# A six-layer encoder trunk on one core: a planner of weight work is replaced by one written order of all instructions and written buffer places

## The chip, the cores and the metric

One core of a Trainium2 chip runs the whole program as one launch. The metric is the device time of one execution in microseconds (us). For the kernel before it is the median of three runs, and one further execution was taken with the hardware profiler; its trace is the source of every view shown here.

The engines go by their short names in the profile's rows: PE is TensorE (PEld its weight loads, which overlap its matmuls), DVE is VectorE, ACT is ScalarE, POOL is GpSimd, SP is the engine that only issues transfers. In the trace each engine's instructions start in the order in which the program issued them; between engines there are semaphores. So an instruction that waits holds back all that stand behind it on its engine.

## The reference, cut to what matters

Two layers, 256 tokens of width 1024, all float32. Each layer has three stages, so there are six in all:

```
for l in range(DEPTH):                                        # DEPTH = 2
    x = LN(ALPHA * x + 0.5 * swiglu(x, ffn_w_in[l, 0], ffn_w_out[l, 0]))
    x = LN(ALPHA * x + mixer_l(x))                            # l = 0: mLSTM, l = 1: window attention
    x = LN(ALPHA * x + 0.5 * swiglu(x, ffn_w_in[l, 1], ffn_w_out[l, 1]))

def swiglu(x, w_in, w_out):                                   # w_in 1024 x 5632, w_out 2816 x 1024
    gu = x @ w_in
    g, u = gu[..., :D_FF], gu[..., D_FF:]
    return (jax.nn.silu(g) * u) @ w_out
```

The order of the stages is thus ffn, mLSTM, ffn, ffn, attention, ffn. Nothing of the mathematics changes here.

## The kernel before, in words

**Splitting.** A float32 operand is held as two parts of the faster type fp32r: `hi`, a rounded copy, and `lo`, what is left. A product is three matmuls (`mm3`): hi by hi, hi by lo, lo by hi. For activations, ScalarE makes `hi` and VectorE makes `lo` straight from the PSUM bank (`split_evac`). For weights the same is done with tiles of 128 x 1024: a load brings 512 KB into a raw tile, ScalarE copies it to `w_hi` (line 204, with a scale line 206), VectorE subtracts to get `w_lo` (line 222, with a scale line 224). Ten places each for `w_hi` and `w_lo` (`RING = 10`) hold weights that are ready for PE; a place comes free when PE has used its tile.

**The ffn stage.** The first 512 columns of g and u are plain products. Most other columns go by a scheme of seven products in place of eight (`seven`): it needs sums of weight blocks, which are made in place in the raw tiles, on VectorE (`tensor_add`, line 236) or by an accumulating transfer issued from POOL (line 240), and sums of transposed inputs (the tiles `S1` to `S4`). Between the products stand blocks of the down projection (`down`, tiles `py`), whose input `h` is silu(g)*u (tile `hh` or `u0`, `u1`), transposed on PE and split again. The stage ends with six down blocks and the layer norm (`tail`, `Norm`).

**Three queues beside PE.** PE's matmuls stand in the order in which the Python code calls them. All other work of the weights is placed between them by a planner that runs while the program is built. The class `Counted` counts every instruction that the model's own code issues. After each one `Weights.run` looks at four lists, H (a `w_hi`), L (a `w_lo`), S (a sum on VectorE) and A (an accumulating transfer); the string `ORDER` gives for each of them the count at which it is due:

```
early = self.made < upto or self.half and self.half[0][0] < upto
next_ = [(o[0], what) for what, o in self.order.items()
         if o and (early or o[0][0] <= self.nc.n) and self.ready(what)]
```

Within one list the order is fixed: `w_lo` tiles are made in the order in which PE will use them. The model's own instructions on VectorE, ScalarE and POOL (evacuations, copies, sums of inputs, norms) stand in the order of the code and cannot pass each other; only weight work is set between them.

**Loads.** SP issues a load as soon as a raw place is free (`Weights.load`, called from `low` and `sum`): four places `w_raw` that live through the whole program, and in an ffn stage six places `s_raw` and two `v_raw` out of that stage's pool. `W.open(pool, end)` at the start of an ffn stage gives those eight to the planner, so before that point only the four `w_raw` places take loads of the coming stage. Each stage has its own pool (`tc.tile_pool(name="ffn")` and so on), closed at its end; four PSUM banks carry the tag `pw` and four `py`, each handed out in turn.

**Names.** `load_x` brings the four halves of the input on ScalarE's queue; `to_xT` transposes x into `xT`; `pending` is the transposing of the second token half, which the next stage does after its first matmuls; `proj`, `scores`, `turn`, `values` and `out_proj` are the parts of the attention stage, `mix`, `divide`, `combine` and `settle` those of the mLSTM. Nearly all instructions bear line 94, a helper that issues them, so they are told apart by their tiles.

Of the kernel before, what the change touches and what calls it, by code (L numbers as in the profile page):

```python
# [1 line left out]

# [27 lines left out]
S_RAW = 6  # L30
V_RAW = 2
RING = 10
QC = [5, 16, 22, 27, 32]
# [5 lines left out]

ORDER = (  # L40
    "H19L0H16L0H33L3H2L4H3H7L2H2L1L5H38H9L0L1S6H2L4H2L0S0H3H3H5L3L3H5L1L12S3S0A8A5H8L3A4H2L2A2H0H2L1H2H0H0H0H0L4L12"
    "L4L3L2L7H6H0H7L2H2H2L1H3L0H1L1S0S0L18H0L7A3A0L6L7H3S17L0S17H3H3L1H0H1A3L4A2L3H2H0H0H2L2H1L3L9L4H1L1L2H7H6L5L7H"
    "2L3L8H2H3H1L4L1H9L3H2L5H11L1L1H1H2L0S2H1A23H5L0S2L0L1H1S2L0A1H5S13H0L3A5H7L1A0H0H1L11L3H8H5L1L4L5H5L1H11L2H2L2"
    "H0H4L2H4H10L6S3H11L2L9L0H0H1S2H1L2A1L3A2S13L5H6L1S8H0H2A6H0L9L4H1H5L1H2L2H2L3L6A5L4H0H0H8H4L2L6L1L14H16H0L2L0H"
    "6H0L1H0L8L11H27L3H14L7H6H6H16L4L1L2H4L2H66H13L30L8H12H6L0H6H47L2H1L6H38L1H1H1L16L15L11H12H5H0L6H13L2L10L15L3H8"
    "H7L40L7H55L8H101L53H60L1H2L0H0H31H1L0L1H4L0L0H0H47L11L11H56H0H0L0L10L0H5L0H6H4L22L4H43L10H1H0L5S1H6L10H11H1L2L"
    "4S9A7L0H0S4L7A4H13S1L5A5H2H4L1A0H3L2H2H3L3H1H2H2L8H3L1L4L1L0H3H19L2L3H0L2L0S2S2H1L4H0H2H17H9L1L8A9L1A4S3L1S5H1"
    "2L4H0H0H1A3L4A2L3H2H0H0L4H3L1H0L9H0L4L2L2H14H10L3L10H9H1L1H0H1L1L1L2H5L2H3L5H5H4L4L1S0H1S3H1L0H14H8A1L3L0L1L0S"
    "2A6H1S2L3H9A11L8A0H0H1L12H2L6H2L0H5L5L5H0H3L3H11H0H0L2L4L10H0L4H6L4L9H6H6S1H1L2S0L0H0L2L0A7A5S9H0S1L14H12A5H2H"
    "7L2L1H2L5H0H3L2L5L6H1A4H4H0H0L8H8L4L4L0L12H15L0H1L0H7H0L1H0L14H1L4L12H32L7H11L3H14L4H0L1H5L16H44L22H2H2L3H0L0L"  # L50
    "6H24L7S3H5S2L5S4A10H1L2A2S12H10H1L3A4L4H1A1L3H0H0H5L1L4H1H5L3H1L4L1L2H13H0L8H0H3L2H2L1L2L1S0S0H14L2H1H3H9L10L2"
    "A3A10L5S0S8H16H0H0L1A2H0L4A2L3H2H0H0H0H0L4L4L9L4H2L5L3H7H4L4H0L6H0L2L1L20H1L1H2L2H2H5L5L11H10H3L1H2H6S1H3A5L2S"
    "1L1L0L1H0S1A6L6H8L7A5S3H3L2H0A0H0H1L1L1L0H20H5H3L2L5L6H11H0H0H0L2L4L10H0L5L2H3L4H19H3L5S0H5A2S0L0L1H0S2A2H9L9L"
    "3S0H15H2A3L0L4H5H5L5H0L5L5H5L1A5H4H0H0H11L1H3L6L2L2L6H18H1H0H1L2L0L7H11L8L7H23L13H14H5L10L2H2H4L6L1H31L5H22H38"
    "L2L2H14L8H21L24H35H0H3L6H1L9L2H41L18H7L14L33H36L27H54L9H37L33H19L27H25L27H80L18H24L4H18H2L4L3H4L18H59H5H3L2L1L"
    "0H1L5H9L6S15H3S14H4L0S2A7L4A1S1H21L4H0H4A0L4H1A1L3H2H0H0H0H0L4L4L9L4L1H2L0H14H8L2H1L2L3L0S2H1H1L7L3H4H3L0S1H4L"
    "13L4A4S5A5S0H29H0H0L1A2H0L4A2L3H2H0H1H1H1L1L4H2L7L4L2H15L1L3H2L9L2H2H14L1L0H0L1H0L3H7H5L5H1L4S0L1H1L6H0H4L18H2"
    "A5S5L0L0S1A6H5L0H3L1A17S2H4L2A0H0L1H0H1L0L11H10H5L5H2L3L6H4H7H0L2H3L1L10H0L6L3S0H1H0H15S3L4L9L0A7A5H3L1S2H3H4L"
    "5L15S0H3H5A0L0H9L3H2L5H0H4L1H1L4L6A5H4H0L5H2H9L4L2L10L2H15H2H0L1L8L0"
)  # L60


class Counted:


    def __init__(self, nc):
        self.nc, self.n, self.then = nc, 0, None
        for name in ("tensor", "vector", "scalar", "gpsimd"):
            setattr(self, name, Engine(self, getattr(nc, name)))

    def __getattr__(self, name):
        return getattr(self.nc, name)

    def load(self, ap, source, engine=None):
        if engine is not None:
            engine.dma_start(ap, source)
        elif isinstance(source, list):
            for k, src in enumerate(source):
                self.nc.sync.dma_start(ap[:, k].rearrange("p (m f) -> p m f", m=src.shape[1]), src)
        else:  # L80
            self.nc.sync.dma_start(ap, source)


class Engine:
    def __init__(self, counted, engine):
        self.counted, self.engine = counted, engine

    def __getattr__(self, name):
        f, c = getattr(self.engine, name), self.counted
        if name.startswith("preload") or "dma" in name:  # L90
            return f

        def call(*args, **kw):
            r = f(*args, **kw)  # L94
            c.n += 1
            if c.then is not None:
                c.then()
            return r
        return call


class Weights:

    def __init__(self, nc, pool, words, plan, after):
        self.nc, self.pool, self.words, self.plan, self.after = nc, pool, words, plan, after
        self.raw, self.parts, self.half = {}, {}, []  # L110
        self.sums = {"S": [], "A": []}
        self.made = self.used = self.room = 0
        self.todo = {tag: [i for i, w in enumerate(words) if w["tag"] == tag] for tag in ("w_raw", "s_raw")}
        self.free = {"w_raw": RAW_BUFS, "v_raw": 0, "s_raw": 0}
        self.spool, self.send = None, 0
        self.uses = [0] * len(words)
        self.order, n = {what: [] for what in "HLSA"}, 0
        for i, (what, step) in enumerate(re.findall(r"([HLSA])(\d+)", ORDER)):
            n += int(step)
            self.order[what].append((n, i))  # L120
        for p in plan:
            self.uses[p["word"]] += 1
        for sums in after.values():
            for w, v in sums:
                if isinstance(v, int):
                    self.uses[v] += 1
        self.first = {}
        for i, p in enumerate(plan):
            self.first.setdefault(p["word"], i)
            for _, v in after.get(i, ()):  # L130
                if isinstance(v, int):
                    self.first.setdefault(v, i + 0.5)

    def open(self, pool, end):

        self.spool, self.send = pool, end
        self.free["s_raw"], self.free["v_raw"] = S_RAW, V_RAW
        self.load()

    def load(self, most=None):  # L140

        nc = self.nc
        n = 0
        while most is None or n < most:
            next_ = []
            for tag, todo in self.todo.items():
                local = todo and todo[0] < self.send
                in_ = tag if self.free[tag] else "v_raw"
                if todo and (local or tag == "w_raw") and (in_ == tag or local and tag == "w_raw") and self.free[in_]:
                    next_.append((self.first[todo[0]], tag, in_))  # L150
            if not next_:
                break
            _, tag, in_ = min(next_)
            i = self.todo[tag].pop(0)
            pool, bufs = {"w_raw": (self.pool, RAW_BUFS), "v_raw": (self.spool, V_RAW), "s_raw": (self.spool, S_RAW)}[in_]
            t = pool.tile([128, D], F32, name=tag, tag=in_, bufs=bufs)
            nc.load(t.rearrange("p (k f) -> p k f", k=self.words[i]["k"]), self.words[i]["src"])
            self.raw[i], self.words[i]["in"] = t, in_
            self.free[in_] -= 1
            n += 1  # L160

    def drop(self, w):
        self.uses[w] -= 1
        if not self.uses[w]:
            del self.raw[w]
            self.free[self.words[w]["in"]] += 1

    def ready(self, what):
        if what == "L":
            return bool(self.half)  # L170
        if what in self.sums:
            q = self.sums[what]
            return bool(q) and all(w in self.raw for w in q[0][1:] if isinstance(w, int)) and not any(
                x[0] == q[0][0] for x in (self.sums["S"] if what == "A" else ()))
        p = self.plan[self.made] if self.made < min(self.room, len(self.plan)) else None
        return p is not None and p["word"] in self.raw and not any(
            x[0] == p["needs"] and (len(x) == 2 or x[1] == p["word"])
            for x in self.half + self.sums["S"] + self.sums["A"])

    def run(self, upto=0):  # L180

        while True:
            early = self.made < upto or self.half and self.half[0][0] < upto
            next_ = [(o[0], what) for what, o in self.order.items()
                     if o and (early or o[0][0] <= self.nc.n) and self.ready(what)]
            if not next_:
                assert not early, (self.made, self.used, self.nc.n)
                break
# [4 lines left out]
    def high(self):  # L193
# [14 lines left out]
        self.made += 1  # L208

    def low(self):  # L210

        nc = self.nc.nc
        i, hi = self.half.pop(0)
        p = self.plan[i]
# [1078 lines left out]
```

## Time and profile before

| what | value |
|---|---|
| median of 3 runs | 936.27 us (934.73 to 937.51) |
| the profiled execution, its own time | 935.19 us |
| its span, first to last instruction | 933.4 us |
| busy: PE, PEld, DVE, ACT, POOL | 914.4, 756.3, 812.3, 574.3, 147.0 us |
| instructions on PE, DVE, ACT, POOL | 4368, 955, 813, 202 |
| moved from memory | 206.65 MB, 223 GB/s over the span |

How to read it: the matmuls overlap each other, so that one of 512 columns stays in flight for about 0.39 us while the next starts 0.23 us after it. PE therefore counts as busy through most of its short waits, and its 98% is not a measure of how much it waits. The weight loads (PEld) do not overlap in that way; their waits are the better list of the moments at which PE had nothing to do.

### The profile page before, as it was taken

What the parts mean: (1) busy time and instruction counts of PE and PEld (TensorE: products, weight loads), DVE (VectorE), ACT (ScalarE), POOL (GpSimd) and SP (SyncE); (2) the same over time, 40 slices, a digit from 0 to 9 for tenths busy, and PEclk for the clock granted to TensorE, in tenths of its full rate; (3) what the DMA queues carried; (4) which work ended last, traced back from release to release, by engine and by line L of the source; (5) the groups of instructions that cost most, each with busy time, mean ns of one, the idle gap of its engine ahead of it and who ended that gap; (6) DMA issues with size and microseconds to landing.
All of it is one profiled execution on the core that took longest, in us unless ns stands there. A gap on an engine that the chain in (4) does not pass through costs nothing.

```text
span 933.4 us, 12378 instructions
## 1 busy us (share of the span) xinstructions
PE 914.4 (98%) x4368; PEld 756.3 (81%) x4368; DVE 812.3 (87%) x955; ACT 574.3 (62%) x813; POOL 147.0 (16%) x202
## 2 busy tenths in 40 slices
PE   9999999999999999999999999999999999999996
PEld 7788888789988788888887888887887787888885
DVE  6899988987687999899889999888888889989986
ACT  6576576546664576765645765765578556676670
POOL 0131111010210112012011111020534302102110
PEclk9999999999999999999999999999999999999999
DMA  8999997646624989998767998975652177999941
GB/s 286 322 274 264 305 270 177 202 136 193 215 99 133 340 235 223 345 254 236 209 209 242 289 258 280 303 154 181 204 177 95 56 285 174 296 314 230 311 116 45
DMA packets 100637, 208.50 MB, mean 223 GB/s; under 512 B 6848, under 2 KB 21200, under 8 KB 100576
## 3 DMA queue, kind: packets, MB, share of 16 engines
q1 hardware_dynamic: 82368, 173.04, 52.9%
q0 software_dynamic: 17632, 33.64, 21.6%
q10 hardware_dynamic: 576, 1.05, 0.3%
q8 instruction: 34, 0.56, 0.2%
q14 instruction: 27, 0.22, 0.1%
HBM read 206.65 MB, written 1.05 MB: 223 GB/s over the span
## 4 chain that ended last, share of the span: by engine, by line
PE 75%; DVE 12%; DMA 5%; ACT 4%; issue 2%; POOL 0%; SPq 0%; DVEq 0%; ACTq 0%
PE pw L94 48%; PE py L94 28%; DVE w_lo L222 5%; DMA s_raw<-in_ffn_w_in_dram 2%; ACT w_hi L204 2%; DVE s_raw L236 1%; DMA w_raw<-in_ffn_w_out_dram 1%; DVE e L94 1%; ACT sc L94 1%; DVE S L94 1%; DVE h_lo L94 1%; DVE rm L94 1%; DVE S_lo L94 0%; DVE o L94 0%; DVE h L94 0%
## 5 line engine op out<-in xcount | busy, mean ns | idle before, releaser
L204 ACT CAST w_hi<-s_raw 128x1024 fp32r<-128x1024 f32 x192 | 197.4, 1051 | 112.6 <-DVE s_raw L236 83.9
L222 DVE TENSOR_TENSOR w_lo<-w_raw,w_hi 128x1024 fp32r<-128x1024 f32 x211 | 253.1, 1219 | 11.0 <-ACT w_hi L204 10.3
L222 DVE TENSOR_TENSOR w_lo<-s_raw,w_hi 128x1024 fp32r<-128x1024 f32 x192 | 229.5, 1220 | 24.3 <-ACT w_hi L204 23.7
L204 ACT CAST w_hi<-w_raw 128x1024 fp32r<-128x1024 f32 x211 | 214.3, 1050 | 44.8 <-DMA w_raw<-in_ffn_w_out_dram 9.8
L94 PE MATMUL pw<-w_hi,xT_hi 128*128 128x512 f32 x480 | 191.4, 399 | 0.7 <-ACT w_hi L204 0.7
L94 PE MATMUL pw<-w_hi,xT_lo 128*128 128x512 f32 x480 | 187.6, 391 | 0.0
L94 PE MATMUL pw<-w_lo,xT_hi 128*128 128x512 f32 x480 | 187.2, 390 | 0.1
L240 POOL DMA_DIRECT2D s_raw<-in_ffn_w_in_dram x64 | 77.7, 1227 | 477.8 <-DVE s_raw L236 183.2
L94 PE MATMUL py<-w_hi,h_hi 128*128 128x512 f32 x352 | 138.3, 393 | 0.3 <-ACT h_hi L94 0.3
L94 PE MATMUL py<-w_hi,h_lo 128*128 128x512 f32 x352 | 137.7, 391 | 0.7 <-DVE h_lo L94 0.6
L94 PE MATMUL py<-w_lo,h_hi 128*128 128x512 f32 x352 | 137.6, 391 | 0.1
L94 PEld LDWEIGHTS pw<-w_hi,xT_lo 128*128 128x128 f32 x480 | 90.1, 188 | 19.5
L94 PEld LDWEIGHTS pw<-w_lo,xT_hi 128*128 128x128 f32 x480 | 90.4, 188 | 18.2 <-DVE w_lo L222 0.9
L94 PEld LDWEIGHTS pw<-w_hi,xT_hi 128*128 128x128 f32 x480 | 90.2, 188 | 18.2 <-ACT w_hi L204 1.1
L94 PE MATMUL pw<-w_lo,S_hi 128*128 128x512 f32 x256 | 100.3, 392 | 1.1 <-DVE w_lo L222 1.1
L94 PE MATMUL pw<-w_hi,S_hi 128*128 128x512 f32 x256 | 99.7, 390 | 0.0
L94 PE MATMUL pw<-w_hi,S_lo 128*128 128x512 f32 x256 | 99.7, 389 | 0.0
L94 PEld LDWEIGHTS py<-w_hi,h_lo 128*128 128x128 f32 x352 | 66.1, 188 | 16.1 <-DVE h_lo L94 2.6
L94 PEld LDWEIGHTS py<-w_lo,h_hi 128*128 128x128 f32 x352 | 66.1, 188 | 15.2 <-DVE w_lo L222 1.8
L236 DVE TENSOR_TENSOR s_raw<-s_raw 128x1024 f32<-128x1024 f32 x64 | 77.4, 1219 | 0.4
L94 PEld LDWEIGHTS py<-w_hi,h_hi 128*128 128x128 f32 x352 | 66.1, 188 | 13.9 <-ACT h_hi L94 0.7
L94 PEld LDWEIGHTS pw<-w_lo,S_hi 128*128 128x128 f32 x256 | 48.1, 188 | 12.8 <-DVE w_lo L222 3.0
(218 smaller groups left out, 1142.3 us busy)
## 6 DMA issues: line engine op xcount, KB each, us to landing
s_raw<-in_ffn_w_in_dram SPq DMA_DIRECT2D x96, 512.0 KB, 7.3
w_raw<-in_ffn_w_out_dram SPq DMA_DIRECT2D x88, 512.0 KB, 6.7
w_raw<-in_ffn_w_in_dram SPq DMA_DIRECT2D x64, 512.0 KB, 5.0
s_raw<-in_ffn_w_in_dram POOLq DMA_DIRECT2D x64, 512.0 KB, 7.5
w_raw<-in_ml_w_in_dram SPq DMA_DIRECT2D x24, 512.0 KB, 4.0
w_raw<-in_ffn_w_in_dram SPq DMA_DIRECT2D x32, 256.0 KB, 6.9
w_raw<-in_at_w_in_dram SPq DMA_DIRECT2D x12, 512.0 KB, 4.1
w_raw<-in_ml_w_out_dram SPq DMA_DIRECT2D x8, 512.0 KB, 4.1
```

The costliest lines, as they stand in the source:

```text
L94: r = f(*args, **kw)
L204: nc.scalar.copy(hi, raw)
L222: nc.vector.tensor_sub(lo, raw, hi.bitcast(F32))
L236: nc.vector.tensor_add(t, t, self.raw[v])
L240: nc.gpsimd.dma_start(t.rearrange("p (k f) -> p k f", k=self.words[w]["k"]), v, accum_op=OP.add)
```

## The change

Every engine call of the model code is now only written down (`Program.ops`), and `Program.issue` at the very end issues all of them in the order given by the string `ORDER`, which is now a list of steps through the 6,654 calls. `Weights.split` writes down the `hi` copy, the `lo` subtraction and the sums of a tile at the point of its use; where they land among the other instructions is settled by `ORDER` alone. The planner (`Weights.run`, `ready`, `high`, `low`, `sum`, `done`, `open`) is gone.

Buffers come from `Rooms`: a buffer has a list of places, and the string for its kind in `SLOTS` names the place of each use in turn (without a string, the places are taken round and round). The eight PSUM banks are one kind, `p`. Raw tiles are one kind per stage: the four `w_raw` places, and in ffn stages eight `s_raw` places beside them. `Stage` puts a stage's buffers at fixed addresses in one region that all stages share, without opening or closing a pool; two neighbouring stages of the same kind (the third and the fourth, both ffn) use the very same buffers. An instruction that overwrites an address waits for the last user of that address, whichever stage it belongs to.

Set side by side in program order, the two programs have the same instructions (calls, by the program's own count): 4368 on PE, 955 on VectorE, 785 on ScalarE, 198 on POOL and 348 transfers on SP's queue. All 4368 matmuls and transposes stand in the same order as before. On VectorE 842 instructions stand at another place in the queue, the mean shift being 3.5 places and the largest 47; on ScalarE it is 691, on POOL 98, on SP 296.

```diff
-S_RAW = 6
-V_RAW = 2
+S_RAW = 8
 RING = 10
+PLACES = {"ffn": (("h_hi", 1024, 2, FR), ("h_lo", 1024, 2, FR))}
+WHOLE = 21800
 ORDER = (
-    "H19L0H16L0H33L3H2L4H3H7L2H2L1L5H38H9L0L1S6H2L4H2L0S0H3H3H5L3L3H5L1L12S3S0A8A5H8L3A4H2L2A2H0H2L1H2H0H0H0H0L4L12"
...
+    "0 5 35 -34 63 -65 4 1 75 -74 1 109 -108 1 87 -99 13 1 123 -135 13 1 136 21 -156 1 1 1 3 1 -3 4 1 -25 189 "
...
+SLOTS = {
...
+    "stats": ("010101010101"),
...
+class Program:
     def __init__(self, nc):
-        self.nc, self.n, self.then = nc, 0, None
-        for name in ("tensor", "vector", "scalar", "gpsimd"):
+        self.nc, self.ops = nc, []
+        for name in ("tensor", "vector", "scalar", "gpsimd", "sync"):
             setattr(self, name, Engine(self, getattr(nc, name)))
+    def issue(self):
+        at, order = 0, []
+        for step in ORDER.split():
+            at += int(step)
+            order.append(at)
...
+        for i in order:
+            f, args, kw = self.ops[i]
+            f(*args, **kw)
...
+        f, ops = getattr(self.engine, name), self.program.ops
+        return lambda *args, **kw: ops.append((f, args, kw))
+class Rooms:
...
+    def take(self, name, shape, dt):
+        places, slots, k = kind = self.kinds[name]
+        kind[2] += 1
+        at = places["0123456789abcdefghijkl".index(slots[k])] if slots else places[k % len(places)]
...
+class Stage:
...
+        places = [self.bass.alloc_sbuf_tensor_at(key.replace(".", "_") + f"_{k}", [128, n], dt,
+                                                 offset=self.start + 4 * (at + k * step)).ap() for k in range(bufs)]
...
 class Weights:
-    def run(self, upto=0):
-        while True:
-            early = self.made < upto or self.half and self.half[0][0] < upto
...
+    def split(self, i):
+        nc, p = self.nc, self.plan[i]
+        k, scale, raw = p["k"], p["scale"], self.load(p["word"])
+        hi = self.rooms.take("w_hi", [128, D], FR)
+        lo = self.rooms.take("w_lo", [128, D], FR)
...
+            nc.scalar.copy(hi, raw)
+            nc.vector.tensor_sub(lo, raw, hi.bitcast(F32))
...
     def take(self, n):
-        i = self.used
         self.used += n
-        self.run(self.used)
-        return [self.parts[j] for j in range(i, i + n)]
+        return [self.split(i) for i in range(self.used - n, self.used)]
...
-    wpool = ctx.enter_context(tc.tile_pool(name="weights", bufs=RING))
+    raws = tiles("w_raw", D, F32, RAW_BUFS)
+    rooms.kind("w_hi", tiles("w_hi", D, FR, RING))
+    rooms.kind("w_lo", tiles("w_lo", D, FR, RING))
+    rooms.kind("p", tiles("p", 512, F32, 8, psum))
...
+    for j, (kind, *_) in enumerate(stages):
+        if j and kind == stages[j - 1][0]:
+            keys.append(keys[-1])
+            stage_rooms.append(stage_rooms[-1])
+        else:
+            keys.append(str(j))
+            stage_rooms.append(new_stage(kind, keys[-1]))
...
-        return psum.tile(list(shape), F32, name="pw", tag="pw", bufs=4)
+        return rooms.take("p", list(shape), F32)
...
-            pool = ph.enter_context(tc.tile_pool(name="ffn", bufs=1))
+            pool = stage_rooms[bound[0]]
...
     pending()
+    nc.issue()
```

More of the change, by code (lines that the diff above doesn't have):

```diff
@@ L84 @@
[L84 to L99, printed above, removed]
-class Weights:
[L108 to L178, printed above, removed]
-    def run(self, upto=0):
-        while True:
-            early = self.made < upto or self.half and self.half[0][0] < upto
[L184 to L188, printed above, removed]
-            _, what = min(next_)
-            self.order[what].pop(0)
-            self.high() if what == "H" else self.low() if what == "L" else self.sum(what)
-    def high(self):
-        nc, i = self.nc.nc, self.made
-        p = self.plan[i]
-        scale, raw = p["scale"], self.raw[p["word"]]
-        hi = self.pool.tile([128, D], FR, name="w_hi", tag="w_hi", bufs=RING)
@@ new lines, with __init__, load @@
+class Weights:
+    def __init__(self, nc, rooms, words, plan, after):
+        self.nc, self.rooms, self.words, self.plan, self.after = nc, rooms, words, plan, after
+        self.raw, self.used = {}, 0
+    def load(self, i):
+        if i not in self.raw:
+            w = self.words[i]
+            self.raw[i] = t = self.rooms.take(w["room"], [128, D], F32)
+            t = t.rearrange("p (k f) -> p k f", k=w["k"])
+            if isinstance(w["src"], list):
+                for k, src in enumerate(w["src"]):
+                    self.nc.sync.dma_start(t[:, k].rearrange("p (m f) -> p m f", m=src.shape[1]), src)
+            else:
+                self.nc.sync.dma_start(t, w["src"])
+        return self.raw[i]
+    def split(self, i):
[3 more added lines that the diff above has]
+        lo = self.rooms.take("w_lo", [128, D], FR)
@@ L251, in done @@
-    def done(self, upto=None):
-        upto = self.used if upto is None else upto
-        for j in [j for j in self.parts if j < upto]:
-            del self.parts[j]
-        self.room = max(self.room, upto + RING)
-        self.run()
+        return [self.split(i) for i in range(self.used - n, self.used)]
 @with_exitstack
@@ L333, in seven @@
         downs(3)
-    ends = {}
     for j, (kind, l, i, _) in enumerate(stages):
+        now[0] = j
         if kind == "ffn":
@@ L379, in trunk_kernel @@
                 rows(at_w_out[0], c)
-        ends[j] = len(words)
     xt = [state.tile([128, D], F32, name=f"x{t}", tag=f"x{t}") for t in range(2)]
@@ L621, in ffn @@
                             early[4 * m + a]()
-                        W.done()
                     if m == 0:
-                        W.open(pool, ends[bound[0]])
                         for t in range(2):
@@ L627, in ffn @@
             else:
-                W.open(pool, ends[bound[0]])
                 for t in range(2):
@@ L770, in ffn @@
                     small_loads()
-            gb = load_ln(lambda name: pool.tile([128, D], F32, name=name, tag="s_raw", bufs=S_RAW), l, n)
+            gb = load_ln(lambda name: rooms.take(f"raw.{keys[bound[0]]}", [128, D], F32), l, n)
             norm = [Norm(t, 2 * ALPHA, 4 * LN_EPS, gb, last) for t in range(2)]
-            todo = list(zip(range(2 * UNITS - TAIL, 2 * UNITS), W.take_rows(TAIL)))
+            todo = list(zip(range(2 * UNITS - TAIL, 2 * UNITS), W.take(TAIL)))
             return tail(y, lambda c, t: pair(hT[c], A, tok(t)), (todo, todo), False, norm,
@@ L1238, in attn @@
                     lows.append((d, o))
-                held = [wo[c][0] for c in wo if c not in CT]
-                W.done(min([W.used - (2 if qpart else 0)] + held))
                 if st < 8:
```

217 lines of the change are left out of this document (120 added, 97 removed), and 189 rows, old and new, of the table ORDER.

## The prediction

> **What bounds the kernel now.** I read the page first, then the chain of what ended last, then the waits of PE's weight loads, then the timelines of the places where PE waits.
>
> ```profile
> span 933.4 us, 12378 instructions
> ...
> PE 914.4 (98%) x4368; PEld 756.3 (81%) x4368; DVE 812.3 (87%) x955; ACT 574.3 (62%) x813; POOL 147.0 (16%) x202
> ```
>
> PE is the bound, and VectorE, idle for 121 us of the span, is close behind. The change leaves PE's instructions and their order alone, so the time can only change by PE's waits and by what follows its last matmul. The busy 98% hides the waits. The chain gives the pace of undisturbed matmuls and the end of the program:
>
> ```profile
> 377.03 2.72 PE py L94 x12
> ...
> 916.39 9.56 PE py L94 x42
> ...
> 925.98 0.70 DVE x L94
> ```
>
> Twelve matmuls of 512 columns take 2.72 us, 0.23 us each. The last ones end near 925.96; the 7.4 us from there to the end of the span are the second half of a norm on VectorE and the stores, the same instructions afterwards. Now the waits of PE's weight loads over the whole span (us in total, times, longest):
>
> ```profile
> PEld pw L94 <- DVE w_lo L222: 3.9, 8, 1.1
> PEld pw L94 <- DVE pr_lo L94: 3.2, 8, 0.7
> PEld py L94 <- DVE h_lo L94: 2.6, 5, 1.1
> PEld pw L94 <- issue: 2.5, 5, 1.0
> PEld pw L94 <- ACT w_hi L204: 2.0, 2, 1.1
> PEld py L94 <- DVE w_lo L222: 1.8, 4, 0.6
> PEld pw L94 <- DVE ident L94: 1.4, 1, 1.4
> PEld pw L94 <- ACT e L94: 1.3, 1, 1.3
> PEld py L94 <- ACT q_hi L94: 1.3, 1, 1.3
> PEld pw L94 <- DVE hh L94: 1.2, 1, 1.2
> PEld py L94 <- ACT h L94: 1.1, 1, 1.1
> PEld py L94 <- DMA x<-in_x_dram: 1.0, 1, 1.0
> PEld py L94 <- DVE w_lo L224: 0.9, 1, 0.9
> PEld pw L94 <- POOL sc L94: 0.9, 1, 0.9
> PEld py L94 <- ACT h_hi L94: 0.7, 1, 0.7
> ```
>
> The fifteen rows are 41 waits and 25.8 us. A weight load can begin while the matmul before it still streams, so I count each wait 0.23 us shorter for PE: 25.8 - 41 x 0.23 = 16.4 us lost. Two waits, for `ident` and for the first half of x (1.9 us by the same count), are the start itself. **14.5 us**, 1.6% of the span, is all that a better order of the other queues can win.
>
> **The change part by part.** Instructions and bytes are equal; raw places are 12 in an ffn stage before and after (4 + 6 + 2 against 4 + 8), and the ten places of `w_hi` and `w_lo` and the eight banks stay. What changes is who stands ahead of whom. For each losing place I give its most, by the count above, and what I take of it.
>
> *The first product, 25 to 50 us.* The waits of this window alone, and VectorE's timeline in it:
>
> ```profile
> PEld pw L94 <- DVE w_lo L222: 2.5, 3, 1.1
> ```
> ```profile
> 29.72 1.22 DVE L236 TENSOR_TENSOR s_raw<-s_raw 128x1024 f32<-128x1024 f32 x1
> 30.85 0.68 DVE L94 TENSOR_TENSOR hh<-sg,pw 128x512 f32<-128x512 f32 x1
> 31.45 1.22 DVE L222 TENSOR_TENSOR w_lo<-s_raw,w_hi 128x1024 fp32r<-128x1024 f32 x1
> ```
>
> With the `hh` wait of 1.2 that lies here, 3.7 us in four waits: 2.8 us lost. The `w_lo` begun at 31.45, for which PE waits, has 25 instructions ahead of it on VectorE; in the written order it has 18. Six of the instructions that make S1 to S4 and the first `hh`, at 0.68 us as `hh`, and the sum of 1.22 us go behind it (one short copy comes ahead): 7 x 0.68 + 1.22 = 6.0 us out of its way, against a wait of at most 1.1. The other waits of the window get room in the same manner. I take 2.3 of 2.8, the rest being transfers that run at full load here (below).
>
> *Entry into the ffn stages at 326, 503 and 775 us.* PE waits for the second `hh`. In the list these are `ACT e` 1.3, one `ACT w_hi` and one `issue` of about 1.0 each, and after each a wait of 0.4 under `py`, `w_lo`: 4.5 us in six waits, 3.1 us lost. The timeline of VectorE has the `hh` of the first of them, SP's shows the loads before it, and two windows the load on the transfers (busy us of PE, PEld, DVE, ACT and POOL, then the clock, the transfers' busy share and GB/s):
>
> ```profile
> 325.20 0.68 DVE L94 TENSOR_TENSOR hh<-sg,pw 128x512 f32<-128x512 f32 x1
> ```
> ```profile
> 306.86 1.90 SPq L81 DMA_DIRECT2D s_raw<-in_ffn_w_in_dram  x4
> ```
> ```profile
> 250.00:300.00 50.00, 48.79 (x258) 41.27 (x257) 40.53 (x80) 25.10 (x46) 5.55 (x5) 1.00 0.31 105
> 300.00:325.00 25.00, 25.00 (x117) 20.53 (x115) 22.99 (x28) 14.48 (x19) 2.76 (x2) 1.00 0.95 319
> ```
>
> The stage's `s_raw` places are opened only at 306.86; before that the transfers are busy for 0.31 of the time, after it for 0.95. In the written order the first of these eight places takes a load 11 places earlier in SP's queue, ahead of a load of the mLSTM's output weights, once the mLSTM's last use of that address is over. So VectorE can have weight work in its idle time (9.5 us in 250 to 300, 2.0 us in 300 to 325). It needs that: in the new order `hh` has more work ahead of it than before, by 2.0, 2.7 and 1.4 us at the three places (splits and a sum come forward, S instructions go back). PE gains only if the idle time is filled by more than that. Since the idle time is about five times as much, I take 2.0 of 3.1. If it is not filled, the same figures turn into a loss: see the second rival.
>
> *The ends of the ffn stages* (`h_lo` 2.6, the other `w_hi` 1.1, `h_hi` 0.7, the fourth `py` `w_lo` 0.6: 5.0 us in eight waits, 3.2 lost). Here the result of the last product has to pass through ScalarE, VectorE, PE's transposes and both again; in the chain of the last stage two pieces of it read
>
> ```profile
> 908.87 0.69 DVE e L94
> ...
> 909.57 0.60 DVE h_lo L94
> ```
>
> and no order shortens these; it can only see to it that nothing stands before them. I take 1.0.
>
> *mLSTM* (`h` 1.1, `w_lo` line 224 0.9: 1.5 lost). The `w_lo` in question stands three places earlier in VectorE's queue. I take 0.8.
>
> *Attention* (`pr_lo` 3.2, `q_hi` 1.3, `sc` 0.9, the other `issue` 1.5: 6.9 us in fourteen waits, 3.7 lost).
>
> ```profile
> 700.00:725.00 25.00, 24.93 (x130) 19.86 (x130) 21.80 (x43) 22.61 (x67) 12.68 (x25) 1.00 0.30 93
> ```
>
> ScalarE is busy for 22.6 of 25 us, VectorE for 21.8, and each step needs the one before; the orders of both queues hardly differ here (the second `pr_lo` of the waits near 721 us is VectorE's instruction 744 before and 742 after). I take a quarter, 0.9. The other `pw`, `w_lo` waits (1.4 us in five) are 0.2 us by the count: nothing.
>
> *The start gets something worse.* Four transfers bring x on ScalarE's queue; then ScalarE evacuates the first transposes; PE needs the last two halves at 10.63.
>
> ```profile
> 0.79 2.20 ACTq L76 DMA_DIRECT2D x<-in_x_dram  x4
> ...
> 5.63 0.58 ACT L94 CAST xT_hi<-py 128x512 fp32r<-128x512 f32 x1 [1.32 <-PE py L94]
> ```
> ```profile
> 10.63 1.04 PE L94 MATMUL py<-ident,x 128*128 128x128 f32 x8
> ```
> ```profile
> DMA to landing us min/median/max: 3.6/6.2/7.8
> ```
>
> In the written order the transfer of the second half of the first 128 tokens stands behind that evacuation, so it is issued not before 5.63 + 0.58 = 6.2 us. Behind it in the queue stand the first `hi` copies, which wait for the issue alone. By the landing times of the four it arrives at 9.8, 12.4 or 14.0: PE waits 0, 1.8 or 3.4 us. I take 1.0, between the best and the median, because three of the four have landed by then and less is in flight. The Trainium skill ("DMA: Bandwidth & Descriptors", Queues, rings and completion order) says that each transfer engine takes turns between the rings of the queues that have work, so that a late transfer on ScalarE's ring need not wait behind SP's weight loads; by that rule the term would be 0 and the time 1 us less. The landing times above, with both rings loaded, do not decide it.
>
> *Free of cost:* POOL's order. Its moved memsets and the norm's power step are under 2 us each, and PE never waits for POOL but for `sc`. If that cover were gone, the power step at a stage's end would hold the norm by one memset.
>
> The sum: 2.3 + 2.0 + 1.0 + 0.8 + 0.9 - 1.0 = 6.0 us less in the span, 927.4. The profiled execution took 935.19 us, 1.8 more than its span, and lies 1.1 below the median of 936.27; against the median I forecast 936.27 - 6.0 = **930.3 us**.
>
> **The rivals.** (What a measurement can tell from no change is about 0.3%, 2.8 us.)
>
> 1. *Nothing gained:* waits go round. Freed waits come back on the next late operand, as ScalarE's `hi` copies are what VectorE's `w_lo` wait for, and attention gives nothing. Half of the recoverable terms and the start's full 3.4: 936.27 - 3.5 + 3.4 = 936.2. For it: PE's small waits have seven different releasers in the list. Against: the two largest losing places have one clear cause each. It includes the case that the shared addresses make a stage wait for the last user of the one before, so that the early loads come no earlier. 14%.
>
> 2. *Slower: evacuations stuck behind weight work.* The order now lets a split stand in front of an `hh`, `e` or `h_lo` that PE needs sooner, counting on the load being there. Where a load lands late, PE waits for the split too. At the three entries that is 2.0 + 2.7 + 1.4 = 6.1 us, and in each of the four ffn stages some four evacuations stand behind one more split than before; at 1.22 us each, half of it felt, 4 x 4 x 0.61 = 9.8. With nothing won but the first product and the entries hit: 936.27 - 2.3 + 1.0 + 6.1 = **941.1**; with the 9.8 as well, 951. It decides itself where transfers are busy for 0.95 of the time, as in 300 to 325: if the earlier loads only push others back. Against it: between 250 and 300 there is room for them. 17%.
>
> 3. *The start fails alone:* 3.4 us there, the rest as forecast: 932.7. 7%.
>
> 4. *Nearly all waits go:* 12 of the 14.5 and no loss at the start: 924.3. An order of all four queues leaves room for it; the chains at the stage ends and in attention speak against. 10%.
>
> **How the numbers follow.** The forecast has 52%; it runs from 927 (attention and the stage ends at a half) to 933 (entries and mLSTM nothing). Cases 3 and 4 are faster too. So faster by over 0.3%: 52 + 7 + 10, less a little of the forecast's upper edge, 0.68. Within 0.3%: rival 1 and that edge, 0.15. Slower: 0.17. The range from 922 (all 14.5 won) to 942 takes in rival 2 at its 941.1, and leaves out its worse cases and little else.
>
> **What would show it.** Right: in the list of PE's weight-load waits, `w_lo` falls from 3.9 to near 1.5 and the `hh`, `e` rows vanish; the first `s_raw` load of the third stage goes out before 300 us; transfers in 250 to 300 are busier than 0.31; DVE's busy time stays 812. The x wait grows by at most 2 us. Attention's `pr_lo` row stays near 3. Wrong: if the sum of the list stays above 23 us, or if `hh` waits grow at 326, 503 or 775 (rival 2), or if the program's time moves while the list does not, since then PE's pace of 2.72 us for twelve matmuls changed, for which I see no reason.

## The result: slower by half a per cent, although PE waits less

| | time before | time after | ratio (95% interval) |
|---|---|---|---|
| median of 7 runs each | 937.51 us | 941.66 us | 1.0048 (1.0028 to 1.0067) |
| profiled execution, its span | 933.4 us | 937.9 us | |

The forecast was 930.3 us, faster; the kernel became 4.2 us slower. The page of the kernel after begins:

```profile
span 937.9 us, 12265 instructions
PE 921.9 (98%) x4368; PEld 757.3 (81%) x4368; DVE 814.0 (87%) x955; ACT 578.4 (62%) x813; POOL 142.3 (15%) x202
```

PE is busy for 7.5 us more than before (914.4) with the same 4368 matmuls. The waits of its weight loads (us in total, times, longest) became shorter in sum, as was forecast:

```profile
PEld p L301 <- DVE pr_lor L301: 4.7, 10, 1.6
PEld p L301 <- DMA x<-in_x_dram: 2.8, 2, 1.8
PEld p L301 <- POOL sc L301: 1.8, 3, 1.2
PEld p L301 <- ACT q_hir L301: 1.7, 2, 0.9
PEld p L301 <- DVE ident L301: 1.5, 1, 1.5
PEld p L301 <- DVE w_lo L301: 1.2, 2, 0.7
PEld p L301 <- ACT t L301: 1.1, 2, 0.8
PEld p L301 <- DVE t L301: 0.8, 4, 0.2
```

The whole list, with four rows of under 0.8 us that are left out here, is 17.4 us in 33 waits; the whole list before, the prediction's fifteen rows and two smaller ones, was 26.5 us in 43. The waits for `pr_lo`, x, `sc` and `q_hi` grew. (`hh`, `e` and `sg` are called `t` now, `h_hi` is `h_hir`, both `pw` and `py` are `p`.) So fewer waits and more time: the pace of PE itself has changed. The timeline of PE in the kernel after shows it in four microseconds (start, duration, operation). Of the two operands behind the arrow the second is stationary, a weight load (PEld) has brought it; the first streams through PE, the moving operand. Here the activations are stationary and the model's weights move:

```profile
61.72 0.40 PE L301 MATMUL p<-w_hi,xT_lo 128*128 128x512 f32 x1
61.95 0.39 PE L301 MATMUL p<-w_hi,h_hir 128*128 128x512 f32 x1
62.19 0.40 PE L301 MATMUL p<-w_lo,h_hir 128*128 128x512 f32 x1
...
64.52 0.39 PE L301 MATMUL p<-w_hi,h_lor 128*128 128x512 f32 x1
64.75 0.39 PE L301 MATMUL p<-w_hi,xT_hi 128*128 128x512 f32 x1
...
65.88 0.39 PE L301 MATMUL p<-w_hi,xT_lo 128*128 128x512 f32 x1
```

The twelve matmuls whose stationary operand is `h` take 2.80 us from 61.95 to 64.75, 0.233 us each; the five steps with `xT` behind them take 1.13 us, 0.226 each. The kernel before, at the same place:

```profile
62.72 0.39 PE L94 MATMUL py<-w_hi,h_hi 128*128 128x512 f32 x1
...
65.44 0.39 PE L94 MATMUL pw<-w_hi,xT_hi 128*128 128x512 f32 x1
```

Twelve `h` steps in 2.72 us, 0.227 each. Over the whole trace, taking the distance from one start to the next for all 512-column matmuls and leaving out those of 260 ns and more (a wait), the 1797 steps into a matmul with `h` or `S` as stationary operand average 233.3 ns after and 227.1 before; the 1434 into one with `xT` stay at 227.6 (227.9 before). That is 1797 x 6.2 ns = 11.2 us. From PE's first start to its last the program takes 3.84 us more; so everything else on PE, its waits above all, became 7.3 us shorter. Behind PE's last matmul there are 0.64 us more, from this piece of the chain:

```profile
931.52 0.16 DVE rs L301
...
931.79 0.96 POOLq L1440
...
932.77 1.43 DVE x L301 x2
...
934.22 0.75 DVE x L301
```

and before:

```profile
927.67 0.15 DVE rs L94
...
927.83 0.72 DVE x L94 x2
...
929.07 0.74 DVE x L94
```

In the kernel before both halves of the norm's first step (the x2) run on VectorE while GpSimd takes the power; in the written order one of them stands behind it. 11.2 - 7.3 + 0.64 = 4.5 us, the difference of the spans.

### The profile page after: what moved, and what is told of

Read it like the earlier page. It is cut to its first block, busy times and chain, and to the rows that moved or that the text cites. A ratio compares the mean times of both kernels' runs of the same rounds, so it can differ in the third digit from the quotient of the medians.

```text
span 937.9 us, 12265 instructions
## 1 busy us (share of the span) xinstructions
PE 921.9 (98%) x4368; PEld 757.3 (81%) x4368; DVE 814.0 (87%) x955; ACT 578.4 (62%) x813; POOL 142.3 (15%) x202
## 3 DMA queue, kind: packets, MB, share of 16 engines
q10 hardware_dynamic: 576, 1.05, 0.3%
HBM read 206.65 MB, written 1.05 MB: 221 GB/s over the span
## 4 chain that ended last, share of the span: by engine, by line
PE 93%; DMA 2%; DVE 2%; ACT 2%; POOL 0%; issue 0%; POOLq 0%; ACTq 0%
PE p L301 93%; DMA x<-in_x_dram 1%; DMA s_raw<-in_ffn_w_in_dram 1%; DVE pr_lor L301 0%; ACT w_hi L301 0%; ACT sc L301 0%; DVE rm L301 0%; DVE x L301 0%; DVE o L301 0%; POOL sc L301 0%; DVE nm L301 0%; ACT q_hir L301 0%; ACT o L301 0%; DVE w_lo L301 0%; POOL sm L301 0%
## 5 line engine op out<-in xcount | busy, mean ns | idle before, releaser
L301 ACT CAST w_hi<-w_raw 128x1024 fp32r<-128x1024 f32 (+1 forms) x168 | 174.3, 1046 | 85.2 <-PE p L301 43.3
L301 DVE TENSOR_TENSOR w_lo<-w_raw,w_hi 128x1024 fp32r<-128x1024 f32 (+1 forms) x168 | 202.4, 1218 | 27.6 <-ACT w_hi L301 27.3
L301 PE MATMUL p<-w_hi,xT_hi 128*128 128x512 f32 x512 | 203.7, 398 | 0.0
L301 PE MATMUL p<-w_hi,xT_lo 128*128 128x512 f32 x512 | 200.1, 391 | 0.0
L301 PE MATMUL p<-w_lo,xT_hi 128*128 128x512 f32 x512 | 199.7, 390 | 0.3 <-DVE w_lo L301 0.3
L301 PE MATMUL p<-w_hi,h_hir 128*128 128x512 f32 x320 | 127.3, 398 | 0.0
L301 PE MATMUL p<-w_lo,h_hir 128*128 128x512 f32 x320 | 126.4, 395 | 0.0
L301 PE MATMUL p<-w_hi,h_lor 128*128 128x512 f32 x320 | 126.2, 395 | 0.0
L301 PE MATMUL p<-w_hi,S_hir 128*128 128x512 f32 x256 | 101.3, 396 | 0.4 <-ACT t L301 0.4
L301 PE MATMUL p<-w_lo,S_hir 128*128 128x512 f32 x256 | 101.2, 395 | 0.0
```

## The experiments

**Is it the place of the tiles?** What distinguishes `h` and `S` from `xT` after the change is where they begin. In the built programs the weights, PE's moving operand, begin at a remainder of 96 bytes modulo 256 in both kernels, and so does `xT`. `h` and `S` begin at remainder 96 in the kernel before and at 64 after it, because the region that all stages share begins there. Three kernels move nothing but places (the second also issues one small memset on GpSimd).

```diff
-WHOLE = 21800
+WHOLE = 21856          # changed kernel: the region starts 224 bytes lower
```

> The changed kernel with its shared stage region begun 224 bytes lower, so that the stage buffers stand at the address remainder (96 of 256 bytes) that they had in the kernel before; the order of issue and the waits in the program are untouched. In the traces, 1823 matmuls whose stationary operand is h or S start 233.3 ns apart after the change against 227 ns before, and those with xT stay at 227. Theory P (place: the pace of a matmul follows from where its stationary tile begins): the h and S matmuls return to 227 ns, 1823 x 6.4 ns = 11.6 us come back, 941.7 - 11.6 = 930 us, while PE's waits stay as in the changed kernel. Theory O (order: the slower pace comes from what the other engines now do beside PE): the pace stays near 233 ns and the time near 941 us.

```diff
           state.tile([128, 8, S], FR, name="xT_lo", tag="xT_lo"))
+    pad = state.tile([128, 56], F32, name="pad", tag="pad")      # kernel before: 224 bytes
+    tc.nc.gpsimd.memset(pad[:, 0:1], 0.0)
```

> The kernel before with one unused 224-byte buffer ahead of its stage pools, so that h and S begin at remainder 64 of 256 bytes, as in the changed kernel; nothing else moves but one tiny memset on GpSimd. Theory P: the h and S matmuls go from 227 to 233 ns and the time rises by 11.6 us, to about 949 us. Theory O: nothing happens, 937.5 us within 0.3%.

```diff
+    tiles("pad", 56, F32, 1)                                     # changed kernel: weights and xT to 64
     raws = tiles("w_raw", D, F32, RAW_BUFS)
```

> The changed kernel with 224 unused bytes ahead of the raw tiles: h and S keep the addresses at which they are slow (remainder 64 of 256 bytes), and the weights and xT are moved to the same remainder 64. If the two operands have to agree, all 512-column matmuls of the ffn stages go at 227 ns and the time is that of the changed kernel with its stage region lowered, 933.6 us within 1.5. If 64 is itself a slow place for a stationary tile, h and S stay at 233 ns and xT joins them: 1434 x 6 = 8.6 us more than the changed kernel before waits give some back, above 945 us.

| kernel | remainder of weights, `h` and `S`, `xT` | step `h`, `S` | step `xT` | time | ratio to before |
|---|---|---|---|---|---|
| before | 96, 96, 96 | 227.1 ns | 227.9 ns | 937.5 us | |
| after | 96, 64, 96 | 233.3 | 227.6 | 941.7 | 1.0048 |
| after, region lowered | 96, 96, 96 | 226.9 | 227.8 | 933.6 | 0.9964 (0.9951 to 0.9976) |
| before, padded | 96, 64, 96 | 233.3 | 227.7 | 945.7 | 1.0089 (1.0074 to 1.0103) |
| after, weights and `xT` moved | 64, 64, 64 | 226.9 | 227.8 | 934.7 | 0.9971 (0.9956 to 0.9985) |

The theory of the order falls: the same order runs at either pace, and so does the old one. The place decides, and the last row says how: `h` and `S` stand where they were slow and are fast, since the weights stand at the same remainder now. Its timeline has twelve `h` steps in 2.72 us again:

```profile
61.98 0.39 PE L301 MATMUL p<-w_hi,h_hir 128*128 128x512 f32 x1
...
64.70 0.39 PE L301 MATMUL p<-w_hi,xT_hi 128*128 128x512 f32 x1
```

Lowering the region and padding the kernel before are worth 8.1 us each in the medians, not 11.6. The pace moved as forecast; but a faster PE runs into its operands again. The gaps of over 0.25 us between PE's matmuls (distance less the usual one of the shape) sum to 8.7 us in the kernel after and to 13.9 with its region lowered: 5.2 us of some 11.5 are given back, and the two profiled executions, 937.9 and 931.7 us, lie 6.2 apart.

**How near must the two be?** Two kernels with the region at other distances, one execution each:

> The changed kernel with its stage region begun at remainder 224, 128 bytes from that of the weights (96). If agreement counts modulo 128 bytes, h and S go at 227 ns; if modulo 256, at 230 to 235 ns. In the map with mixed places no tile but xT went at a clean 227, so 256 is the likelier.

> The same with the region at remainder 160, 64 bytes from the weights'. If agreement counts modulo 64 bytes, h and S go at 227 ns; otherwise at 230 to 235.

At a distance of 128 bytes the `h` and `S` steps average 232.5 ns, at 64 bytes 233.2, `xT` 228 in both. Neither 64 nor 128 bytes is the period. It is no longer than 256, for `xT` begins 96 bytes into a block of 512 in the kernel after and the weights 352, and these agree modulo 256 only. All weights stand at one remainder, so these runs do not tell whether a matmul's own moving operand counts or that of the matmul before it, beside which its weight load runs (the load starts 3 ns after that matmul in the median).

A map with all eight remainders in one program came first:

> The changed kernel with 32 bytes between the h and S tiles, so that these stand at all eight remainders of 256 in steps of 32 bytes (h_hi 64 and 96, h_lo 128 and 160, S1_hi 192, S1_lo 224, S2_hi 0, S2_lo 32, S3_hi 64, S3_lo 96, S4_hi 128, S4_lo 160), the moving weights at 96 as ever. Only the pace by tile is read. Theory P with period 64: the tiles at 96, 160, 224 and 32 go at 227 ns, those at 0, 64, 128 and 192 at 233. Theory P with period 256 (stationary and moving operand must agree): only 96 goes at 227, the others between 230 and 236. The attention's q, at 224 in the changed kernel and at 0 in the one before, goes at 232 in both, which speaks for the second. Theory O: one pace for all, 233.

> The same, and the weights, which are the moving operand, begin at remainder 128 and xT at 160. If the distance between moving and stationary operand decides, the whole map shifts by 32 bytes: the tile at 128 (h_lo's first, S4_hi) is now the fast one and xT, 32 bytes above the weights, takes what the tile 32 bytes above the weights took before (that at 128). If the stationary operand's own place decides, the tiles keep the paces that they have with the weights at 96, and xT takes that of 160.

It did not do what it was made for. In the first the `h` and `S` tiles average 229.6 to 234.1 ns, those at 96 too (231.1 for the second place of `h_hi`, 233.0 for `S3_lo`); in the second 230.5 to 235.4, and no tile at 128 is fast. Where tiles at several remainders follow one another, none keeps a pace of its own. A step depends on its neighbour too: in the first map a step of `h` or `S` in agreement takes 234.9 ns behind one that is 64 bytes off (119 steps), and one that is 64 bytes off takes 229.6 behind one in agreement (160 steps). I can't say why. What can be read is `xT`, which all stands at one place: 32 bytes from the weights it goes at 233.2 ns, where at agreement it went at 228.0, and the single execution took 947.7 us against 939.5.

**The start and the attention.** On top of the lowered region, the x load goes to its old place, and unused bytes bring `kp`, `q`, `v`, `pr` and `sc` to remainder 96:

```diff
-ORDER: ... x(1,0) ... x(1,1) ... first xT_hi ... x(0,1)
+ORDER: ... x(1,0), x(0,1) ... x(1,1) ... first xT_hi
         if tag not in self.tags:
+            self.top += {"kp_hi": 24, "pr0_hi": 32}.get(tag, 0)
```

> The changed kernel with its stage region lowered to remainder 96 and two more edits that are read apart in the trace. The load of the second half of the first tokens is issued right after the first load, as in the kernel before: if the place of this load behind the evacuation is why PE waits for x, the waits for x of the first 13 us (3.2 us in the list of weight-load waits, 2.7 us lost) go to about 1.0, and 1.6 to 2 us of the time with them; if the load is late because the transfers are busy with weights, nothing changes. Unused bytes in the attention stage put kp, q, v, pr and sc at remainder 96 as well: if agreement of the places decides there too, the q and v matmuls go from 232 to 227 ns (about 100 of them against w, 0.5 us); if the attention's pace has another cause (its busy ScalarE), they stay at 232. Sum: 933.6 - 1.8 - 0.5 = 931.3 us.

It took 932.8 us, 0.9950 (0.9932 to 0.9967) of before: not to be told apart from the kernel with the region alone by its time. The trace tells: the second x wait, 1.8 us lost at 12.7 us, is gone; the first, 0.87 and now 1.43, lies anywhere between 0.85 and 1.87 us in the traces of this study. The `q` steps against the weights went from about 233 to 229. Both edits did what they should, and PE's gaps fell from 13.9 to 11.5 us. That the two profiled executions (931.7 and 932.1 us) do not show it is in large part explained by the next place.

**Where the rest of the order's gain went.** With agreeing places the order gains about 4 us in the medians (1.7 us between the two profiled executions), not 6, and PE's gaps are as long as before the change: 13.9 us with the region lowered against 13.6. They stand elsewhere. One of them, in the kernel with the early x load, read from the timeline of ScalarE and then PE:

```profile
810.84 1.05 ACT L304 CAST w_hi<-w_raw 128x1024 fp32r<-128x1024 f32 x1
815.06 2.00 ACT L304 CAST w_hi<-s_raw 128x1024 fp32r<-128x1024 f32 x2 [3.17 <-DMA s_raw<-in_ffn_w_in_dram]
816.97 0.62 ACT L304 ACTIVATE t<-t 128x512 f32<-128x512 f32 x1
817.50 1.05 ACT L304 COPY t<-p 128x512 f32<-128x512 f32 x2
```
```profile
815.81 0.39 PE L304 MATMUL p<-w_hi,h_lor 128*128 128x512 f32 x1
818.11 0.50 PE L304 MATMUL p<-w_hi,S_hir 128*128 128x512 f32 x1 [1.91 <-ACT t L304]
```

ScalarE stands idle for 3.17 us at a `w_hi` whose load is late, and behind it wait two copies of `t` that would free the bank which PE needs. In the kernel before these copies stand 8 and 11 places earlier in the queue. That is the mechanism of rival 2, at a place that I had not named.

The gap, 2.07 us, is not all that this place costs in this execution. Behind it PE's granted clock is at half of full speed for 3.4 us. Two windows show it (after the busy times of the five engines the clock, the transfers' share and GB/s):

```profile
818.00:820.00 2.00, 1.89 (x5) 1.56 (x6) 0.78 (x1) 0.55 (x2) 0.00 (x0) 0.63 1.03 405
820.00:822.00 2.00, 2.00 (x6) 1.53 (x6) 0.16 (x1) 1.04 (x1) 0.00 (x0) 0.52 0.69 263
```

Ten matmuls there start 0.29 to 0.43 us after one another, 1.7 us more than usual in sum, which the sum of the gaps leaves out. With the region alone the gap at this place was 1.59 us, and the clock stayed at 1.00.

A first attempt put stretches of the old order back, and one kernel the whole of it:

> The previous kernel with two short stretches of ScalarE's and VectorE's queues (28 to 31 instructions each) put back into the relative order of the kernel before: one around 552 us, where PE waited 1.21 us for hh with three splits more ahead of it on VectorE, and one around 818 us, where PE waited 2.07 us for a bank that two ScalarE copies of t had to empty, the copies standing behind two w_hi copies whose load was late (ScalarE idle for 3.17 us). Theory (an evacuation stuck behind weight work): both waits go, the time falls by up to 3.2 us to 929.6 us. Rival (the load itself is late): PE waits as long a little later, for w_hi or w_lo, and the time stays at 932.8.

> The previous kernel (places in agreement everywhere, the x load early) with the instructions of the attention stage on VectorE, ScalarE, GpSimd and the loads on SP put back into the relative order that they have in the kernel before, as far as the new places allow (six stand one place off). In the attention (633 to 740 us) PE's gaps of over 0.25 us came to 3.05 us before and to 5.70 us in the previous kernel (the longest 1.35, 1.11, 0.67, 0.64, 0.60). Theory: the new order of the attention is what costs; they fall to near 3.1 us and the waits for pr_lor from 4.8 to near 3.2 us, the time by 2.6 to 930.2 us. Rival: the shared addresses and the loads that come late into them cost; then the gaps stay at 5.7 us and the time at 932.8.

> Both of the last two edits. If both theories hold, 932.8 - 2.6 - 3.2 = 927.0 us; if only the stretches hold, 929.6; if only the attention, 930.2; if neither, 932.8.

> The places of the previous kernel (all in agreement at remainder 96 of 256 bytes) under the order of the kernel before, on all queues (93 of the 2286 instructions beside PE stand elsewhere, one to a few places, since the new places forbid their old one). The pace of PE is that of the kernel before, so what is left of the difference to it comes from order or places. If the order made the gain of the changed kernel with agreeing places over the kernel before (about 4 us), this one is at the time of the kernel before, 937.4 us within 1.5; if the shared places with their earlier loads made it, it is near 933.

All four missed: 943.7 and 956.5 us (one execution each), 965.9 (ratio 1.0304, 1.0280 to 1.0327) and 1016.6 us (1.0839, 1.0809 to 1.0869). The waits aimed at are gone in the first, but two others of 3.1 and 4.3 us stand some 20 us behind the moved stretches; in the last, PE waits for `t` by VectorE alone 38.7 us:

```profile
PEld p L275 <- DVE t L275: 38.7, 16, 5.4
PEld p L275 <- ACT h_hir L275: 14.0, 3, 6.0
```

Part of their time is the clock: it averages 0.991, 0.988, 0.985 and 0.974 over their profiled executions, and 0.996 to 0.999 in the runs of all other kernels. Behind each of their sixteen gaps of 3.1 us or more it is at half for some microseconds, behind those of 2 to 2.6 us in some cases and not in others. Why the gaps came is argued, not shown: `SLOTS` was written for one order, and under another an instruction may find its place still in use. A mixture of two orders may cost in itself, and these runs do not separate the two. The last of them leaves open how much of the gain is order and how much the shared places. So the next kernels keep every place and move only the weight work that stands ahead:

```diff
 ScalarE, 818 us:
-  w_hi, w_hi, silu, copy t, copy t
+  copy t, silu, copy t, w_hi, w_hi
 VectorE, 552 us (the last t is hh):
-  w_lo A, w_lo B, t, t, w_lo C, t
+  w_lo A, t, t, w_lo C, t, w_lo B
 attention: four w_hi (ScalarE, 674 to 721 us) and two w_lo (VectorE) behind the casts, exponentials
 and reductions that they stood ahead of; one pr_lo ahead of three small steps
```

> The moves at 552 and 818 us alone: by the theory 3.1 us less, about 929.7, with the attention's gaps as they were; by the rival no gain.

> The attention's moves alone: by the theory 2.8 us less than 932.8, about 930.0, with the gaps at 552 and 818 us as they were; by the rival no gain.

> The kernel with agreeing places and the early x load, every place as it is, with a dozen instructions moved in the written order: weight work that stood ahead of something PE needs sooner goes behind it. In the attention four w_hi copies on ScalarE (ahead of the kp and sc work at 675, 676, 681 and 684 us, their products read only at 726 us and later) with two of their w_lo, one w_hi at 720 us, and one pr_lo goes ahead of two small steps; at 552 us one w_lo goes behind hh; at 818 us the two copies of t and a silu go ahead of two w_hi whose load is late. Theory (evacuations stuck behind weight work): PE's gaps there (0.64, 0.46, 1.11, 1.35, 1.21, 2.07 us) shrink by 1.0 + 1.1 + 0.7 + 1.1 + 2.0 = 5.9 us; 932.8 - 5.9 = 926.9 us, or 929 if a third of it comes back elsewhere. Rival (any move against places written for another order makes new waits, as the coarse moves did): 932 or more.

Both together took **928.7 us, 0.9902 (0.9880 to 0.9924) of before**, the lowest median of the study. Of the 5.9 us hoped for 4.1 came. Single executions of the parts took 929.0 (the two places) and 932.1 (the attention): nearly all of the gain is that of the two places, 3.8 where 3.1 were hoped for, and the attention's share, 0.3 to 0.8 us where 2.8 were hoped for, cannot be told from nothing by these times. In the place shown above ScalarE now runs

```profile
809.33 0.58 ACT L304 COPY t<-p 128x512 f32<-128x512 f32 x1
810.74 0.63 ACT L304 ACTIVATE t<-t 128x512 f32<-128x512 f32 x1 [0.83 <-DVE t L304]
811.28 0.57 ACT L304 COPY t<-p 128x512 f32<-128x512 f32 x1
812.48 2.00 ACT L304 CAST w_hi<-s_raw 128x1024 fp32r<-128x1024 f32 x2 [0.63 <-DMA s_raw<-in_ffn_w_in_dram]
```

and PE's gap there is gone, the half clock with it (1.00 in this kernel up to PE's last matmul); a gap of 0.88 us for `t` stands some 10 us behind. In the attention the work in front was the weights of the output product, which PE reads only after 725 us. One of their `w_hi` stood between the exponentials whose sums GpSimd waits for (ScalarE's and GpSimd's timelines of the kernel with the early x load):

```profile
680.84 0.46 ACT L304 ACTIVATE sc<-p,nm 128x256 f32<-128x256 f32 x1
...
681.41 1.05 ACT L304 CAST w_hi<-w_raw 128x1024 fp32r<-128x1024 f32 x1
682.36 0.47 ACT L304 ACTIVATE sc<-p,nm 128x256 f32<-128x256 f32 x1
...
683.91 0.20 POOL L304 TENSOR_TENSOR sm<-sm,es 128x4 f32<-128x4 f32 x1 [21.89 <-ACT sc L304]
```

With it behind them, the wait for `sc` at 688 us (1.11 us lost) is gone, as are those for `kp` (0.64 and 0.46); the `pr_lo` wait of 1.35 became 0.51, and a new one of 1.13 us for `sc` took part of it back. The attention's gaps fell from 5.70 to 3.76 us.

## Why the prediction was wrong, point by point

The step that failed is in the first part: "The change leaves PE's instructions and their order alone, so the time can only change by PE's waits and by what follows its last matmul." It can also change by where the operands begin. The last sentence of the prediction named half of the sign ("if the program's time moves while the list does not, since then PE's pace of 2.72 us for twelve matmuls changed") with "I see no reason"; the reason stood in the diff, in the line that gives every stage buffer an address. The addresses of all tiles of both programs could have been laid side by side beforehand, as their orders were. The term that was missing is +11.2 us of pace, +8.1 us of time.

That "the same instructions" stand behind the last matmul was not enough either: their order differs, and that was wrong, by 0.64 us.

The terms, by PE's gaps of over 0.25 us, each gap under the part to which the prediction counted its place:

| part | forecast of the gain | before | after | region lowered | weight work behind |
|---|---|---|---|---|---|
| start | -1.0 | 0.94 | 2.76 | 3.70 | 1.75 |
| first product | 2.3 | 2.85 | 0 | 0 | 0 |
| ffn entries | 2.0 | 2.63 | 0 | 0.35 | 0 |
| ffn, the rest | 1.0 | 2.64 | 1.05 | 4.09 | 2.20 |
| mLSTM | 0.8 | 1.53 | 0 | 0 | 0 |
| attention | 0.9 | 3.05 | 4.86 | 5.76 | 3.76 |
| sum | 6.0 | 13.64 | 8.67 | 13.90 | 7.71 |

- **First product, entries, mLSTM**: right in sign and taken too small. The cause given for the entries shows the signs that it was to show, though no run isolates it: the transfers between 250 and 300 us, which had a busy share of 0.31 and 105 GB/s, now have 0.46 and 165, VectorE is busier, and the first `s_raw` of the third stage goes out at 265 us, not at 307:

```profile
250.00:300.00 50.00, 50.00 (x265) 42.92 (x264) 43.10 (x84) 26.68 (x49) 3.37 (x5) 1.00 0.46 165
...
265.37 0.39 SPq L301 DMA_DIRECT2D s_raw<-in_ffn_w_in_dram  x1
```

  Rival 2's place, the entries, was thus wrong: its 941.1 us is met by the measured 941.7 by chance.
- **Start**: right in kind, and 1.5 us were lost at that load where 1.0 were forecast. It was issued late and took 6.1 us to land:

```profile
6.63 6.12 DMA x<-in_x_dram
```

  That is near the median of the issues before (6.2). By the rule of the Trainium skill ("DMA: Bandwidth & Descriptors", Queues, rings and completion order) the term would have been 0; as I applied it, it does not agree with this row. With the load early that wait is gone.
- **Attention**: wrong in sign. That "the orders of both queues hardly differ here" had been read from `pr_lo`, which hardly moved. The copies of the output weights had moved by up to 32 places, and I had not looked at them.
- **The rest of the ffn stages**: the old waits went and new ones came, by the mechanism of rival 2, which I had priced at the entries. At the slower pace most of them are hidden (1.05 us), at the faster one they show (4.09).

The Trainium skill ("TensorE: Matmul & The Clock Gate", Step-by-step: what each phase is for) says that PE reads its streaming operand and the operand of its weight loads through two independent ports. The steps here depend on the two places together (227 ns at 96 and 96 and at 64 and 64, 233 at 96 and 64), which speaks for an effect of one read on the other in these programs; no run shows it directly, or by which way.

## What to carry to other kernels

When a change moves buffers, compare their addresses as you compare the order, and read PE's pace from start to start by operand before reading its waits: here 6 ns on each of 1800 matmuls outweighed all the waits that a new order won. Moving a region by 224 bytes was worth 8 us without touching an instruction. Weight work pulled ahead in a queue is free only as long as nothing behind it is needed before its load has come; look at what was moved forward, not only at what was moved back. A wait of PE of 2 us or more may cost more than its length: read the granted clock behind it.

## What the runs showed of the hardware that I had not expected

In the streams of `h`, `S` and `xT` with the weights a 512-column fp32r matmul follows the one before after 227 to 228 ns where stationary and moving operand begin at the same remainder modulo 256 bytes, and after 232 to 233 ns at distances of 32, 64 and 128 bytes. The weight load itself takes the same (188 and 187 ns in the median); between its end and the start of its matmul lie 36 ns with agreeing places and 44 without. A slower PE hides part of its own cost: 11 us of pace were 8 us of time, in both directions. And a gap of 2.07 us on PE was followed by 3.4 us at half the granted clock, 1.7 us more; each of the sixteen gaps of 3.1 us or more was followed by such a stretch. Length alone does not decide it: a gap of 2.28 us in the kernel with all at 64 left the clock at 1.00.
